# A first feed-forward group of three plain pairs, with the token sums made during its third: five seven-product pairs instead of six

## The chip, the cores and the metric

The kernel runs on one core of a Trainium2 chip. The metric is the device time of one execution in microseconds (us); the time before is the median of three runs. One further execution was taken with the hardware profiler, and every row shown here is from it. A core has a matrix engine (TensorE, called PE in the rows; its weight loads have an engine name of their own, PEld), VectorE (DVE), ScalarE (ACT), GpSimd (POOL), and SyncE (SP), which issues the DMA transfers here. Each engine works through its own list of instructions in order and waits at an instruction until what it needs is there.

## What is computed

One decoder layer on 512 tokens of width 1024, in float32. The part that matters here is the feed-forward block at the end, with `D_FF = 2816`:

```python
h = rmsnorm(x, norm_mix_w[l])
...
x = x + mix @ w_o[l]
h = rmsnorm(x, norm_ffn_w[l])
x = x + (jax.nn.silu(h @ w_gate[l]) * (h @ w_up[l])) @ w_down[l]
return rmsnorm(x, final_norm_w)
```

Ahead of it stand a gated MLP and a sparse attention group, which the change does not touch.

## The kernel before

Every product of float32 values is made from three matmuls (`mm3`, lines 112 to 115): each operand is split into a high part (a copy rounded to `fp32r`, made on ACT, line 81) and a low part (the rest, a subtraction on DVE, line 78), and high times high, high times low and low times high are added up in PSUM. `h2h` and `h2l` are the high and low parts of the normalized tokens, `wg_h`, `wg_l`, `wu_h`, `wu_l` those of gate and up weights, `ah` and `al` those of the activations that go into the down projection.

The 2816 features are cut into 11 pairs of two 128-feature blocks. Pairs are gathered into groups, `FFN_GROUPS = (2, 3, 3, 3)`. For each group the kernel makes gate and up of its pairs one after another and then the down projection of the whole group (`down`). A pair's gate and up is made in one of two ways:

- `plain_pair`: for gate and for up, two feature blocks by eight 128-row slices of the contraction by three matmuls of 512 token columns: 96 matmuls. DVE makes four low parts of weights (128x1024), two products silu(gate) times up (line 710), four sums of 256 columns (line 700) and two low parts of activations. Pair 0 is made in the same way, its first block still inside the stage before.
- `seven_pair`: gate and up, the two halves of the contraction and the two halves of the tokens make a 2x2 block product, done with seven block products (M1 to M7) in place of eight, each of two feature blocks by four slices by three matmuls of 256 columns: 168 matmuls. It needs sums and differences of the weights (`vec2`, line 804), seven low and seven high parts of weights, and sums and differences of the token blocks, `th` and `tl`. M1 takes the plain tokens; M5 is the first that needs `th`.

The token sums are made once by `token_sums` (lines 770 to 788): eight DVE additions and subtractions (lines 776 and 781) of 128x1024, four ACT copies to `th` and four DVE subtractions to `tl`. The call stands after the pairs of group 0, ahead of that group's down projection.

`down` is itself a seven-product scheme (M1, M2, M5, M6, M3, M7, M4 in this order). For every product and pair of the group it splits one 128x512 block of the down weight (`wd0M` to `wd10M`; high on ACT, low on DVE), partly after a difference made in place (lines 924, 927 and 930), and issues 6 matmuls of 512 columns: 42 per pair. After each product but M2, DVE adds two 128x512 results, one per half of 256 tokens, to the residual `x2` (line 890). A result bank (`pA`, `pC`) can be started anew only when its addition has read it, so PE waits on line 890 if DVE is late. M2 has banks of its own (`pB`), kept over all groups.

Raw weights arrive by DMA in three buffers of 1 MB (tag `wr`), used in turn; the split parts go through eight buffers of 128x1024 (tag `wh`), also in turn. A plain pair uses all eight, so the splits of the next pair follow PE at a distance of one pair. The activations of a group stay until its down projection is over; `ACT_HOMES` says in which pool each of them lies. Pool `P` has three buffers and also lends two to `token_sums` for the sums (`tok`).

The order on each engine is made by the framework's scheduler from the order in which the code is written, so instructions of one pair stand among those of the next.

Of the kernel before, what the change touches and what calls it, by code (L numbers as in the profile page):

```python
# [18 lines left out]
P = 128  # L19
# [10 lines left out]
NFB = DFF // P  # L30
C_U, C_V, C_Q, C_KC, C_KS, C_KW, C_G = 0, 512, 1024, 1536, 1792, 2048, 2304
NG = 24
FFN_GROUPS = (2, 3, 3, 3)
SEVEN = (2, 3, 5, 6, 8, 9)
ACT_HOMES = (("xa", "xa", "b8", "P"), ("P", "P", "P", "b8", "xa", "xa"))
START = (("S", 0), ("T", 0), ("W", 0), ("K", 0), ("S", 1), ("T", 1), ("W", 1), ("S", 2), ("K", 1), ("T", 2),
         ("W", 2), ("S", 3), ("K", 2), ("T", 3), ("W", 3), ("K", 3))
BANKS = (3, 2, 2, 1)
# [5 lines left out]
def hybrid_gmlp_nsa_kernel(  # L44
# [18 lines left out]
    def b8(shape, dt, name):  # L63
        return bp.tile(shape, dt, tag="b8", name=name)
# [12 lines left out]
    def sub(o, a, hi, eng=None):  # L77
        return (eng or nc.vector).tensor_tensor(out=o, in0=a, in1=hi.bitcast(F32), op=OP.subtract)  # L78

    def copy_a(o, a):  # L80
        return nc.scalar.activation(o, a, AF.Copy)  # L81
# [35 lines left out]
    def bcast_row(vec, n, name, tag=None):  # L117
        t = (cp if tag else kp).tile([P, DM if tag else n], F32, name=name, tag=tag or name)[:, :n]
        nc.sync.dma_start(t, bass.AP(tensor=vec.tensor, offset=vec.offset, ap=[[0, P], [1, n]]))
        return t  # L120
# [574 lines left out]
    def keep_acts(p, sg, ss):  # L695
        ah, al = act_tile(f"ah{p}"), act_tile(f"al{p}")
        copy_a(ah[:, 0:3], sg[:, 1:4])
        for o, x, y, op in ((ss[:, 0], sg[:, 0], sg[:, 2], OP.add), (ss[:, 2], sg[:, 1], sg[:, 0], OP.subtract),
                            (ss[:, 1], ss[:, 0], sg[:, 1], OP.subtract), (ss[:, 3], sg[:, 3], ss[:, 1], OP.subtract)):
            nc.vector.tensor_tensor(out=o, in0=x, in1=y, op=op)  # L700
        sub(al[:, 0:3], sg[:, 1:4], ah[:, 0:3])
        copy_a(ah[:, 3:7], ss)
        sub(al[:, 3:7], ss, ah[:, 3:7])
        acts.append((ah, al))


    def gate_act(sg, e, pg):
        own = sg[:, 2 * e:2 * e + 2].rearrange("p a c -> p (a c)")
        nc.scalar.activation(own, pg[0], AF.Silu)
        nc.vector.tensor_tensor(out=own, in0=pg[1], in1=own, op=OP.mult)  # L710
# [4 lines left out]
    def gate_up(f, part=None):  # L715
        if part == 0:
            ws = [load_cols(w, 0, KD, f * P, P, f"w{'gu'[a]}{f}", spare=True, behind=mixed[-1])
                  for a, w in ((0, w_gate), (1, w_up))]
            gu[f] = ws, [bank("S", [P, S], f"gu{f}{a}") for a in range(2)]
        elif part is None:  # L720
            raw = wp.tile([P, 2, KD, P], F32, tag="wr", name=f"wgu{f}_r", bufs=NPAIR)
            ws = []
            for a, w in ((0, w_gate), (1, w_up)):
                nc.sync.dma_start(raw[:, a], w[:, f * P:(f + 1) * P].rearrange("(k p) f -> p k f", p=P))
                ws.append(halves(raw[:, a], [KD, P], f"w{'gu'[a]}{f}", last_norm))
            gu[f] = ws, [bank("G", [P, S], f"gu{f}{a}") for a in range(2)]
        cut = slice(0, S) if part is None else slice(part * 256, part * 256 + 256)
        for (hi, lo), z in zip(*gu[f]):
            for k in range(KD):
                mm3(z[:, cut], hi[:, k], lo[:, k], h2h[k // 4][:, k % 4, cut], h2l[k // 4][:, k % 4, cut],  # L730
                    k == 0, k == KD - 1)
        return gu[f][1]
# [17 lines left out]
    def plain_pair(p):  # L750
        sg, ss = t4([P, 4, 256], F32, f"sg{p}"), t4([P, 4, 256], F32, f"ss{p}")
        z = {}
        for a, r in enumerate(pair_raw(p)):
            for kh in range(2):
                hi, lo = halves(r[:, 4 * kh:4 * kh + 4], [4, 256], f"w{'gu'[a]}{p}{kh}")
                for e in range(2):
                    if kh == 0:
                        z[e, a] = bank("G", [P, S], f"gu{p}{a}{e}")
                    for k in range(4):
                        c = slice(e * P, (e + 1) * P)  # L760
                        mm3(z[e, a], hi[:, k, c], lo[:, k, c], h2h[kh][:, k], h2l[kh][:, k],
                            kh + k == 0, kh == 1 and k == 3)
        for e in range(2):
            gate_act(sg, e, (z[e, 0], z[e, 1]))
        keep_acts(p, sg, ss)
# [4 lines left out]
    def token_sums():  # L770
        rs = []
        for a in range(2):
            r = bp.tile([P, 2, 4, 256], F32, tag="P", name=f"tok{a}", bufs=NP)
            for c in range(2):
                cut = slice(c * 256, c * 256 + 256)
                nc.vector.tensor_tensor(out=r[:, c], in0=h2h[a][:, :, cut].bitcast(F32),
                                        in1=h2l[a][:, :, cut].bitcast(F32), op=OP.add)
            rs.append(r)
        y11, y12, y21, y22 = rs[0][:, 0], rs[0][:, 1], rs[1][:, 0], rs[1][:, 1]
        for o, x, y in ((y11, y12, y11), (y12, y22, y12), (y22, y22, y11), (y21, y21, y22)):  # L780
            nc.vector.tensor_tensor(out=o, in0=x, in1=y, op=OP.subtract)
        for a in range(2):
            hi, lo = b8([P, 2, 4, 256], F32R, f"th{a}"), b8([P, 2, 4, 256], F32R, f"tl{a}")
            for c in range(2):
                copy_a(hi[:, c], rs[a][:, c])
                sub(lo[:, c], rs[a][:, c], hi[:, c])
            TH.append(hi)
            TL.append(lo)
# [107 lines left out]
    def down(gi, pairs):  # L896
# [34 lines left out]

        last_group = gi == len(FFN_GROUPS) - 1

# [23 lines left out]
    onw = None  # L957
    for gi, n in enumerate(FFN_GROUPS):
        acts.clear()
        homes[:] = ACT_HOMES[min(gi, 1)]  # L960
        for p in range(p0, p0 + n):
            if p == 0:
                gate_act(sg0, 1, gate_up(1))
                keep_acts(0, sg0, ss0)
            elif p in SEVEN:
                seven_pair(p)
            else:
                plain_pair(p)
        if gi == 0:
            token_sums()  # L970
        if gi == len(FFN_GROUPS) - 1:
            onw = bcast_row(final_norm_w, DM, "onw", tag="wb")
        down(gi, range(p0, p0 + n))
        p0 += n
# [49 lines left out]
```

## Time and profile before

| | us |
|---|---|
| median of three runs | 630.02 |
| the three runs | 630.36, 626.82, 630.02 |
| the profiled execution | 626.75 |
| its span, first to last instruction | 625.0 |
| PE busy in the span | 597.8 |
| DVE busy in the span | 473.0 |
| ACT busy in the span | 329.2 |

The times in the rows are counted from the start of the span. A matmul is pipelined: its row is longer than the distance to the next one, so the pace of PE is read from the starts of matmuls, and that of DVE from the starts of its instructions.

### The profile page before, as it was taken

To read this page: it belongs to the slowest core of one execution; us is meant where nothing else is said; L and a number is where in the kernel's file an instruction comes from. 1 tells how busy PE (TensorE), PEld (TensorE's weight loads), DVE (VectorE), ACT (ScalarE), POOL (GpSimd) and SP (SyncE) were. 2 spreads that over 40 slices of the span, in tenths; PEclk is the share of its full clock that TensorE was granted. 3 is DMA by queue.
4 is the path that set the end of the run, shared out by engine and by line. 5 is a ranking of instruction groups with operands and counts; after the bars stand their busy time and mean duration, and the time that the engine had idled before them with its cause. 6 is when DMAs were issued, how large, how long until landed. Compare 5 with 4: busy or idle time off the path is not lost.

```text
span 625.0 us, 8610 instructions
## 1 busy us (share of the span) xinstructions
PE 597.8 (96%) x3244; PEld 503.6 (81%) x3244; DVE 473.0 (76%) x801; ACT 329.2 (53%) x587; POOL 68.3 (11%) x113
## 2 busy tenths in 40 slices
PE   8999999999999999999958999999999999999994
PEld 5878778787788777888836998888998888998883
DVE  5752778647998967546798898597898597897696
ACT  6653367649877874354341564343464343464354
POOL 3100100015432671000000000000000000000001
PEclk9999999999999999999969999999999999999999
DMA  8451635532000021093004406006415005425003
GB/s 288 144 141 54 179 105 152 184 127 112 1 2 1 1 71 31 17 297 125 1 0 135 136 23 247 1 1 202 136 44 226 0 11 191 136 75 196 1 0 134
DMA packets 52698, 61.38 MB, mean 98 GB/s; under 512 B 3361, under 2 KB 43313, under 8 KB 52658
## 3 DMA queue, kind: packets, MB, share of 16 engines
q1 hardware_dynamic: 52080, 59.80, 29.3%
q10 hardware_dynamic: 578, 1.05, 0.5%
q8 instruction: 25, 0.41, 0.3%
q14 instruction: 15, 0.12, 0.1%
HBM read 58.74 MB, written 2.10 MB: 97 GB/s over the span
## 4 chain that ended last, share of the span: by engine, by line
PE 67%; DVE 19%; DMA 6%; ACT 4%; POOL 2%; issue 2%; POOLq 0%; ACTq 0%; SPq 0%; DVEq 0%
PE gu L114 6%; PE gu L115 6%; PE gu L113 6%; PE o L651 3%; PE ptp L631 3%; PE s L557 3%; DVE x L890 2%; PE po L115 2%; PE po L114 2%; PE gA L115 2%; PE po L113 2%; PE gA L113 2%; PE gA L114 2%; DMA wu_r<-in_w_up_dram 2%; DVE wu_r L804 2%
## 5 line engine op out<-in xcount | busy, mean ns | idle before, releaser
L168 POOL TENSOR_TENSOR rstd_y<-s_y,mhalf 128x1 f32<-128x1 f32 x4 | 3.0, 747 | 355.2 <-DVE s_y L165 350.5
L562 ACT ACTIVATE P<-P,nm 128x128 f32<-128x128 f32 (+3 forms) x64 | 35.5, 559 | 4.8 <-DVE nm L560 4.6
L84 POOL TENSOR_SCALAR P<-P,sm 128x128 f32<-128x128 f32 (+3 forms) x64 | 34.0, 551 | 32.8 <-DVE sm L569 19.6
L560 DVE CUSTOM_DVE_ANT_0 P<-s,maskw 128x128 f32<-128x128 f32 (+3 forms) x64 | 29.5, 481 | 4.2 <-PE s L557 3.6
L651 PE MATMUL o<-PT,Vt 128*128 128x512 f32 x80 | 31.1, 439 | 0.2
L78 DVE TENSOR_TENSOR PT<-ptp,PT 128x512 fp32r<-128x512 f32 x40 | 26.6, 685 | 5.7 <-ACT PT L81 5.5
L113 PE MATMUL gu<-h2h,wg_h 128*128 128x512 f32 x72 | 28.1, 390 | 0.0
L114 PE MATMUL gu<-h2l,wg_h 128*128 128x512 f32 x72 | 28.1, 390 | 0.0
L115 PE MATMUL gu<-h2h,wu_l 128*128 128x512 f32 x72 | 28.0, 389 | 0.0
L115 PE MATMUL gu<-h2h,wg_l 128*128 128x512 f32 x72 | 28.0, 389 | 0.0
L113 PE MATMUL gu<-h2h,wu_h 128*128 128x512 f32 x72 | 28.0, 389 | 0.0
L114 PE MATMUL gu<-h2l,wu_h 128*128 128x512 f32 x72 | 28.0, 389 | 0.0
L631 PE MATMUL ptp<-ident,P 128*128 128x128 f32 x160 | 25.7, 275 | 2.0 <-POOL P L84 1.9
L81 ACT ACTIVATE PT<-ptp 128x512 fp32r<-128x512 f32 x40 | 22.6, 593 | 8.5 <-PE ptp L631 8.1
L557 PE MATMUL s<-KAB,QS 128*128 128x512 f32 (+2 forms) x96 | 27.0, 374 | 0.0
L631 PEld LDWEIGHTS ptp<-ident,P 128*128 128x128 f32 x160 | 19.8, 140 | 7.4 <-POOL P L84 3.2
L890 DVE TENSOR_TENSOR x<-pA,x 128x512 f32<-128x512 f32 x32 | 21.8, 685 | 1.9 <-PE pA L115 1.9
L651 PEld LDWEIGHTS o<-PT,Vt 128*128 128x128 f32 x80 | 14.8, 188 | 7.9 <-ACT PT L81 4.1
L557 PEld LDWEIGHTS s<-KAB,QS 128*128 128x128 f32 x96 | 16.3, 189 | 2.0 <-DVE nm L560 0.3
L81 ACT ACTIVATE sg<-gA 128x512 f32<-128x512 f32 x12 | 7.1, 589 | 19.7 <-PE gA L115 19.7
L804 DVE TENSOR_TENSOR wg_r<-wg_r,wu_r 128x1024 f32<-128x1024 f32 x12 | 14.7, 1223 | 2.8 <-DMA wu_r<-in_w_up_dram 2.4
L81 ACT ACTIVATE ah<-ss 128x1024 fp32r<-128x1024 f32 x11 | 11.6, 1059 | 8.9 <-DVE ss L700 8.9
(735 smaller groups left out, 2088.0 us busy)
## 6 DMA issues: line engine op xcount, KB each, us to landing
wd_r<-in_w_down_dram SPq DMA_DIRECT2D x11, 1024.0 KB, 4.7
wg_r<-in_w_gate_dram SPq DMA_DIRECT2D x10, 1024.0 KB, 7.6
wu_r<-in_w_up_dram SPq DMA_DIRECT2D x10, 1024.0 KB, 5.6
wo_r<-in_w_o_dram SPq DMA_DIRECT2D x8, 512.0 KB, 4.7
x_sb<-in_x_dram SPq DMA_DIRECT2D x4, 512.0 KB, 8.8
wv_r<-in_w_in_dram SPq DMA_DIRECT2D x4, 512.0 KB, 7.2
wu_r<-in_w_in_dram SPq DMA_DIRECT2D x4, 512.0 KB, 4.8
w1k_r<-in_cmp_k_w_dram SPq DMA_DIRECT2D x4, 512.0 KB, 4.2
```

The lines of the kernel that those rows point to most:

```text
L81: return nc.scalar.activation(o, a, AF.Copy)
L84: nc.gpsimd.tensor_scalar(out=o, in0=a, scalar1=s, scalar2=1.0, op0=OP.mult, op1=OP.mult)
L113: nc.tensor.matmul(ps, lhsT=sh, rhs=mh, start=first, stop=False, skip_group_check=more)
L114: nc.tensor.matmul(ps, lhsT=sh, rhs=ml, start=False, stop=False, skip_group_check=more)
L115: nc.tensor.matmul(ps, lhsT=sl, rhs=mh, start=False, stop=last, skip_group_check=more)
L557: nc.tensor.matmul(sb, lhsT=q, rhs=KAB[kv][:, a, b0:b0 + nbr, :n], start=(a == 0), stop=(a == 1))
L560: nc.vector.tensor_tensor_reduce(out=pr, in0=sb[:, br], in1=maskw[:, S - n:], scale=-0.125, scalar=BIG, op0=OP.add, op1=OP.min, accum_out= ...
L562: e = nc.scalar.activation(pr, pr, AF.Exp, bias=nm[b], scale=-1.0, accum_out=sm[b])
L631: nc.tensor.transpose(pt[:, hh], src, ident)
L651: nc.tensor.matmul(of, lhsT=Vt[:, b0 + br, j, kv], rhs=PTs[u][:, a], start=(first and a == 0), stop=False)
L804: nc.vector.tensor_tensor(out=o, in0=x, in1=y, op=op)
L890: nc.vector.tensor_tensor(out=x2[t][:, c], in0=src, in1=x2[t][:, c], op=OP.add)
```

## The change

Groups are now of 3, 3, 2 and 3 pairs. Pair 2 moves into group 0 and is made plain; pairs 3 and 4 (seven) and 5 (plain) make group 1, pairs 6 (seven) and 7 (plain) group 2, and 8 and 9 (seven) and 10 (plain) group 3, as before. So six pairs of seven products become five. `token_sums` is called after pair 1, ahead of pair 2. The homes of the first group's activations get two entries more, both in pool `P`.

```diff
-FFN_GROUPS = (2, 3, 3, 3)
-SEVEN = (2, 3, 5, 6, 8, 9)
-ACT_HOMES = (("xa", "xa", "b8", "P"), ("P", "P", "P", "b8", "xa", "xa"))
+FFN_GROUPS = (3, 3, 2, 3)
+SEVEN = (3, 4, 6, 8, 9)
+ACT_HOMES = (("xa", "xa", "b8", "P", "P", "P"), ("P", "P", "P", "b8", "xa", "xa"))
...
             else:
                 plain_pair(p)
-        if gi == 0:
-            token_sums()
+            if p == 1:
+                token_sums()
         if gi == len(FFN_GROUPS) - 1:
             onw = bcast_row(final_norm_w, DM, "onw", tag="wb")
         down(gi, range(p0, p0 + n))
```

On DVE at the end of pair 1, before the change. `sg1`, `ss1`, `al1` are pair 1's gated results, their sums and their low part, `wd0M6` the split of pair 0's down weight for M6, `pA00` and `pA01` the two banks of M1.

```order
L710 TENSOR_TENSOR sg1_2782<-gu111_2863,sg1_2782 128x512
L78 TENSOR_TENSOR wd0M6_3011<-wd0_r_2940,wd0M6_3011 128x512
L700 TENSOR_TENSOR ss1_2783<-sg1_2782 128x256
L78 TENSOR_TENSOR wd1M6_3015<-wd1_r_2942,wd1M6_3015 128x512
L700 TENSOR_TENSOR ss1_2783<-ss1_2783,sg1_2782 128x256
L78 TENSOR_TENSOR al1_2909<-sg1_2782,ah1_2908 128x768
L700 TENSOR_TENSOR ss1_2783<-sg1_2782,ss1_2783 128x256
L776 TENSOR_TENSOR tok0_2918<-h2h0_1179,h2l0_1181 128x1024 x2
L78 TENSOR_TENSOR al1_2909<-ss1_2783,ah1_2908 128x1024
L776 TENSOR_TENSOR tok1_2921<-h2h1_1180,h2l1_1182 128x1024 x2
L781 TENSOR_TENSOR tok0_2918<-tok0_2918 128x1024
L890 TENSOR_TENSOR x2_1_1172<-pA00_2950,x2_1_1172 128x512
```

On DVE at the same place, of the change. `wu21` is the last quarter of pair 2's weights, `wd0M1` the split of pair 0's down weight for M1.

```order
L710 TENSOR_TENSOR sg1_2782<-gu111_2863,sg1_2782 128x512
L700 TENSOR_TENSOR ss1_2783<-sg1_2782 128x256
L78 TENSOR_TENSOR wu21_l_3035<-wu2_r_2944,wu21_h_3034 128x1024
L700 TENSOR_TENSOR ss1_2783<-ss1_2783,sg1_2782 128x256
L78 TENSOR_TENSOR al1_2909<-sg1_2782,ah1_2908 128x768
L700 TENSOR_TENSOR ss1_2783<-sg1_2782,ss1_2783 128x256
L776 TENSOR_TENSOR tok0_2918<-h2h0_1179,h2l0_1181 128x1024 x2
L78 TENSOR_TENSOR al1_2909<-ss1_2783,ah1_2908 128x1024
L776 TENSOR_TENSOR tok1_2921<-h2h1_1180,h2l1_1182 128x1024 x2
L781 TENSOR_TENSOR tok0_2918<-tok0_2918 128x1024
L78 TENSOR_TENSOR wd0M1_3082<-wd0_r_3076,wd0M1_3082 128x512
```

The sums keep their place behind pair 1's gated results. Before, the splits for M1, M2, M5 and M6 stood ahead of them and the first addition of M1's result (line 890) among them; now pair 2's weights stand ahead of them, and the first splits for M1 among them.

On DVE at the end of group 0's down projection, of the change: `pA00` and `pA01` are here the banks of M4, the last product, `wd2M4` the split of pair 2's down weight for it, `w3M1` and `w3M5` the weights of pair 3's first and second product.

```order
L78 TENSOR_TENSOR wd2M4_3275<-wd2_r_3080,wd2M4_3275 128x512
L890 TENSOR_TENSOR x2_0_1171<-pA00_3091,x2_0_1171 128x512
L890 TENSOR_TENSOR x2_0_1171<-pA01_3101,x2_0_1171 128x512
L78 TENSOR_TENSOR w3M1_l_3305<-wg3_r_3300,w3M1_h_3304 128x1024
L804 TENSOR_TENSOR wg3_r_3300<-wg3_r_3300,wu3_r_3302 128x1024
L804 TENSOR_TENSOR wu3_r_3302<-wu3_r_3302 128x1024
```

On DVE at the same place between the groups of three pairs before the change (group 1 to pair 5; `pA10` and `pA11` hold M7 and then M4, `pC11` M3):

```order
L890 TENSOR_TENSOR x2_1_1172<-pC11_3774,x2_1_1172 128x512
L890 TENSOR_TENSOR x2_0_1171<-pA10_3703,x2_0_1171 128x512
L78 TENSOR_TENSOR w5M1_l_3915<-wg5_r_3910,w5M1_h_3914 128x1024
L890 TENSOR_TENSOR x2_0_1171<-pA11_3713,x2_0_1171 128x512
L804 TENSOR_TENSOR wg5_r_3910<-wg5_r_3910,wu5_r_3912 128x1024
L890 TENSOR_TENSOR x2_0_1171<-pA10_3703,x2_0_1171 128x512
L804 TENSOR_TENSOR wu5_r_3912<-wu5_r_3912 128x1024
```

The first product's weights, which between groups of three pairs stand ahead of the last three additions, stand behind all of them at the end of the new group 0.

## Rows read from the trace of the kernel before

**Rows 1.** The page, part 1: busy time, share of the span, instructions.

```profile
PE 597.8 (96%) x3244; PEld 503.6 (81%) x3244; DVE 473.0 (76%) x801; ACT 329.2 (53%) x587; POOL 68.3 (11%) x113
```

**Rows 2.** PE's waits, 300 to 346 us: waiting instruction, releaser, us, times, longest.

```profile
PE pA L113 <- DVE x L890: 6.8, 2, 4.0
PE gC L113 <- ACT w2M_h L81: 1.9, 1, 1.9
PE gC L115 <- DVE w2M_l L78: 0.8, 1, 0.8
```

**Rows 3.** Windows: busy time (count) of PE, PEld, DVE, ACT, POOL; PEclk, DMA share, GB/s.

```profile
318.00:328.40 10.40, 6.38 (x17) 4.01 (x15) 10.40 (x13) 4.23 (x4) 0.00 (x0) 0.51 0.00 0
342.00:345.40 3.40, 3.19 (x15) 3.19 (x16) 2.18 (x3) 1.89 (x2) 0.00 (x0) 0.51 0.02 5
```

**Rows 4.** PE's timeline, first matmuls of pieces: start, duration (us), engine, line, out<-in, shapes.

```profile
303.20 0.39 PE L113 MATMUL gu<-h2h,wu_h 128*128 128x512 f32 x1
...
305.93 0.39 PE L113 MATMUL pA<-wd0M,ah 128*128 128x512 f32 x1
...
352.14 0.28 PE L113 MATMUL gA<-th,w2M_h 128*128 128x256 f32 x1
...
357.90 0.28 PE L113 MATMUL gA<-th,w2M_h 128*128 128x256 f32 x1
...
360.78 0.28 PE L113 MATMUL gA<-h2h,w3M_h 128*128 128x256 f32 x1
...
380.93 0.40 PE L113 MATMUL gu<-h2h,wg_h 128*128 128x512 f32 x1
...
402.72 0.39 PE L113 MATMUL pA<-wd2M,ah 128*128 128x512 f32 x1
...
431.61 0.28 PE L113 MATMUL gA<-h2h,w5M_h 128*128 128x256 f32 x1
...
452.40 0.28 PE L113 MATMUL gA<-h2h,w6M_h 128*128 128x256 f32 x1
...
473.81 0.40 PE L113 MATMUL gu<-h2h,wg_h 128*128 128x512 f32 x1
```

**Rows 5.** DVE's timeline behind pair 1, 306 to 313 us (idle before, releaser in brackets).

```profile
306.13 0.69 DVE L710 TENSOR_TENSOR sg<-gu,sg 128x512 f32<-128x512 f32 x1 [0.32 <-PE gu L115]
306.73 0.68 DVE L78 TENSOR_TENSOR wd0M<-wd_r,wd0M 128x512 fp32r<-128x512 f32 x1
307.33 0.42 DVE L700 TENSOR_TENSOR ss<-sg 128x256 f32<-128x256 f32 x1
307.67 0.68 DVE L78 TENSOR_TENSOR wd1M<-wd_r,wd1M 128x512 fp32r<-128x512 f32 x1
...
308.61 0.95 DVE L78 TENSOR_TENSOR al<-sg,ah 128x768 fp32r<-128x768 f32 x1
309.48 0.42 DVE L700 TENSOR_TENSOR ss<-sg,ss 128x256 f32<-128x256 f32 x1
309.81 2.35 DVE L776 TENSOR_TENSOR tok<-h2h,h2l 128x1024 f32<-128x1024 f32 x2
312.08 1.22 DVE L78 TENSOR_TENSOR al<-ss,ah 128x1024 fp32r<-128x1024 f32 x1
```

**Rows 6.** DVE's timeline, two starts of a seven-product pair; last row: the tile wu_r's landings.

```profile
331.17 0.68 DVE L78 TENSOR_TENSOR wd0M<-wd_r,wd0M 128x512 fp32r<-128x512 f32 x1
...
337.28 1.23 DVE L804 TENSOR_TENSOR wg_r<-wg_r,wu_r 128x1024 f32<-128x1024 f32 x1
338.54 1.23 DVE L804 TENSOR_TENSOR wu_r<-wu_r 128x1024 f32<-128x1024 f32 x1
340.93 1.23 DVE L78 TENSOR_TENSOR w2M_l<-wu_r,w2M_h 128x1024 fp32r<-128x1024 f32 x1 [1.17 <-ACT w2M_h L81]
...
427.32 1.23 DVE L78 TENSOR_TENSOR w5M_l<-wg_r,w5M_h 128x1024 fp32r<-128x1024 f32 x1 [0.94 <-ACT w5M_h L81]
...
DMA to landing us min/median/max: 5.2/5.6/5.7
```

## The prediction

> **What bounds the kernel now.** I read the page's busy times first: PE is busy for 597.8 of 625.0 us [rows 1], so the time is PE's work plus PE's gaps. A pipelined matmul's busy time hides its pace, so I read the pace from starts: twelve matmuls of 512 columns lie between 303.20 and 305.93, 0.2275 us each; 48 of 256 columns lie between 352.14 and 357.90, 0.120 us each [rows 4]. Then I went piece by piece through the feed-forward part and set each piece against this pace.
>
> - Plain pair 4, 96 matmuls, 380.93 to 402.72: 21.79 us. No gap.
> - Seven-product pair 3, 168 matmuls, 360.78 to 380.93: 20.15 us, against 168 x 0.120 = 20.16. No gap.
> - Down projection of three pairs (126 matmuls, 28.67 us at this pace) and pair 5 (20.16), 402.72 to 452.40: 49.68 us, 0.85 more than the pace. Pair 6, 452.40 to 473.81: 21.41, so 1.25 more [rows 4].
> - Down projection of group 0 (84 matmuls, 19.11) and pair 2 (20.16), 305.93 to 360.78: 54.85 us against 39.27. Here 15.6 us are lost.
>
> The view of waits names them: 6.8 us in two waits for the addition of line 890, then 1.9 and 0.8 for the weights of pair 2 [rows 2], 9.5 in all. The other 6.1 are slow matmuls: the granted clock is 0.51, so the lower level of 1.2 GHz, from 318.0 to 328.4 and from 342.0 to 345.4 [rows 3], each behind such waits. The cause stands in DVE's timeline: behind pair 1 come the token sums [rows 5], and the additions that free PE's banks are queued among and behind them. DVE is the bound of this stretch, and PE of all others.
>
> **The change part by part.** *What goes.* The 15.6 us of this stretch. What becomes of DVE's debt there is worked out below as a new loss.
>
> *Pair 2 plain instead of seven.* 72 matmuls fewer, but wider: 21.79 - 20.16 = +1.6 us on PE. The Trainium skill ("TensorE: Matmul & The Clock Gate", section on the back-to-back issue gap) has a sustained pace of 131 ns at 512 columns and 81 at 128; halfway by columns that is about 98 at 256, an estimate from that page. By it a plain pair would be 96 x 131 = 12.6 us, a seven-product one 168 x 98 = 16.5, and this term -3.9 in place of +1.6. The measured starts differ from that page by 70%, and the measurement decides.
>
> DVE loses ten instructions and ACT six with pair 2's seven products; neither is on the path there, so I count nothing for them. The DMA bytes are the same.
>
> *Pair 2 itself, with the sums beside it.* The listings show pair 2's four weight splits on DVE ahead of the sums; the last starts when PE leaves pair 1, and PE needs it three quarters into pair 2, 16 us later. So pair 2 should run without a gap, from 305.93 to 327.72. The four ACT copies to `th` lie beside it; the last waits in ACT's queue behind two splits for M2, whose `wh` buffers PE frees three quarters into pair 2, near 322.3. That makes it ready near 324.7, about when DVE comes to it.
>
> *Group 0's down projection.* DVE's cost per instruction, by distance of starts: 0.60 us at 512 columns, 0.34 at 256, 0.87 at 768, 1.14 at 1024 [rows 5]. From its start at 306.13 to the last addition of the new group 0 DVE has: three products of line 710 (1.8), seven sums of line 700 (2.4), four low parts of activations (4.0), pair 2's last split (1.1), 12 sum instructions (13.6), 21 splits (12.6), differences of lines 924, 927, 930 (3.4 + 3.6) and 14 additions (8.4): 50.9 us. PE has 21.79 + 28.67 = 50.5 in the same time. So they are nearly even, and DVE enters the down projection with no lead. Laying the listed order out by these costs, I get DVE at the second line 710 of pair 2 at 328.1, PE through M2 at 336.3 (0.4 late), waiting 0.75 for pair 1's split for M5, which stands behind three differences, and about 0.8 in M6 and M3; M4 ends at 358.1 instead of 356.4. Loss: 1.7. Bounds: 0.4 (50.9 - 50.5) and 6.8, the waits on line 890 now [rows 2].
>
> *Start of pair 3.* In the steady state the first product's weights are split at 427.32, four us before PE wants them at 431.61 [rows 4, 6]. Now that split stands behind the last two additions, the very last of which waits for PE's last matmul: addition 358.3 to 358.9, split to 360.05. PE issues two matmuls of M1 and waits 1.8 us. Then the chain that pair 2 shows, two differences and an ACT copy (337.28, 338.54, 340.93 [rows 6]), gives M5's high part at 363.45 and its low part at 364.6, while PE ends M1 at 362.75: 0.7 and 1.0 us. M6 and M2 lose another 0.3. Loss: 3.8. Bounds: 0.85, the steady state, and 8.8, all of the 15.6 but the waits on line 890.
>
> *Which pairs follow which.* Pairs 3 and 4 now stand as 2 and 3 did; pair 6, which lost 1.25 as second of its group, becomes a first. I credit half: -0.6 (0 to -1.25).
>
> *Group of two pairs.* DVE has 14 additions and 14 splits (16.8) and the differences (2.3 + 2.4), 21.5 us, against 19.1 on PE. But the listing of the change has the splits for M1, M2 and M5 and all differences done before pair 7 ends, which covers the 2.4 missing. The up weights of pair 8 take the buffer of pair 6's down weights; DVE last reads that about 10.9 us into the down projection. A load lands 5.6 us later [rows 6], at 16.5, and DVE, ACT and DVE bring M5's weights to PE at about 22.0, when it has finished M1 (19.1 + 2.9). I take +0.3, bounds 0 and 2.7 (what pair 2 loses there now, rows 2).
>
> **The sum:** -15.6 + 1.6 + 1.7 + 3.8 - 0.6 + 0.3 = -8.8 us. On the profiled execution's 626.75 that is 618.0. The median of the runs shown, 630.02, lies 3.3 above it. If that difference sits elsewhere, the new median is 621.2; if it sits in the waits that go, 618.0. I take the middle, 619.5.
>
> **The rivals.** *The lower clock comes back.* Behind waits of 1.9 and 0.8 us within four us the clock was at 0.51 for 3.4 us [rows 2, 3], which cost 1.7. The new waits at the start of pair 3, 1.8, 0.7 and 1.0 within seven us, are like them, but more spread out. One such stretch gives -7.1; the full 6.1 of now gives -2.7. The middle is about 622 on the median's scale. The Trainium skill (the same page, on how the clock gate bites in real kernels) has the clock fall behind long gaps of PE; the waits here were short and it fell, so its rule does not exclude this.
>
> *DVE holds its lead.* If the engines slide so that both new losses shrink to the lower bounds (0.4 and 0.85), the sum is -13.4 and the time 613.3 to 616.6. For it: the balance of 50.9 against 50.5. Against it: the fixed order of the last split.
>
> *The page's pace.* With -3.9 for pair 2 the sum is -14.3, some 613. The rows exclude it all but wholly.
>
> *DVE's debt is larger than 50.9 (slower).* That sum has no time for hand-overs from ACT. DVE idles 0.94 and 1.17 for such copies [rows 6]. With 0.6 us in each of the 21 splits the debt is 13 us, all of it PE's waits on line 890 or on splits, since DVE has no lead. Add the 6.1 of low clock and 3.8 at pair 3: 22.9 in place of 5.5, sum +8.6, time 635 to 638. It decides from a new loss of 15 us on. Against it: in the 20 us behind pair 1 DVE waits nearly nowhere now [rows 5], as the copies run ahead while DVE is late.
>
> **How the numbers follow.** Forecast 0.66, low clock 0.14, DVE's lead 0.10, the page's pace 0.01, larger debt 0.09, of which half ends slower. A difference of 1%, 6.3 us, is about what can be told from none here. Faster by more: the forecast nearly whole (0.60), lead and page (0.11), a third of the low clock (0.05): 0.76. Slower by more: 0.05. Same: 0.19. The range runs from 612.5 (the lead, on the profiled execution's scale, with a margin) to 627.5 (low clock in full, -2.7 on the median). The scale of the runs, 3.3 us, is in it.
>
> **What would show it.** PE's waits on line 890 in group 0 gone or under 1 us; pair 2 from about 305.9 to 327.7 without a gap; `gA` of pair 3 waiting 1 to 2 us for `w3M_l`, then `gC` for `w3M_h` and `w3M_l`; pair 3 ending near 382; clock 1.00 throughout group 0; down projection of pairs 6 and 7 at about 19.1 us. Wrong: waits on line 890 of several us in the new group 0, clock near 0.5 there, or pair 8 starting with waits for `wu_r`.

## The result and the profile after

The changed kernel takes 622.39 us (median of 4 runs, 620.21 to 622.87), the kernel before 628.96 (4 runs, 626.82 to 630.36). The ratio is 0.9892 with a 95% interval of 0.9852 to 0.9932: faster, by about 1.1%. Whether it is more or less than 1% the interval (0.7 to 1.5%) leaves open. The profiled execution took 620.21 us, its span is 618.5. That is 6.5 below the span before; the prediction had 8.8.

The page's busy times (part 1) and the granted clock of the 40 slices, after the change:

```profile
PE 597.3 (97%) x3172; PEld 498.2 (81%) x3172; DVE 463.5 (75%) x791; ACT 324.5 (52%) x581; POOL 68.3 (11%) x113
...
PEclk9999999999999999999999999999999999999998
```

PE has 72 matmuls fewer and the same busy time [rows 1]: a plain pair has fewer but wider ones. What changed is the gaps, and the stretches at half the clock, in which busy time grows without more work. PE's waits from 300 to 372 us, the part that lost 15.6 us before (columns as in [rows 2]):

```profile
PE gA L115 <- DVE w3M_l L78: 1.3, 1, 1.3
PE gC L113 <- ACT w3M_h L81: 1.0, 1, 1.0
PE gC L115 <- DVE w3M_l L78: 0.8, 1, 0.8
PE pC L114 <- DVE wd1M L78: 0.3, 1, 0.3
PE pC L113 <- ACT wd1M L81: 0.2, 1, 0.2
```

The 6.8 us for line 890 [rows 2] are gone, and three waits for the first weights of pair 3 have come. The window that had half the clock before [rows 3] now lies in pair 2:

```profile
318.00:328.40 10.40, 10.40 (x48) 8.61 (x47) 10.40 (x12) 6.15 (x9) 0.00 (x0) 1.00 0.00 0
```

PE is busy for all of it at clock 1.00, with DVE busy throughout as well. The first matmuls of the pieces, in PE's timeline (compare [rows 4]):

```profile
306.55 0.39 PE L113 MATMUL gu<-h2h,wg_h 128*128 128x512 f32 x1
...
328.31 0.39 PE L113 MATMUL pA<-wd0M,ah 128*128 128x512 f32 x1
...
359.23 0.39 PE L113 MATMUL gA<-h2h,w3M_h 128*128 128x256 f32 x1
...
383.83 0.28 PE L113 MATMUL gA<-h2h,w4M_h 128*128 128x256 f32 x1
...
404.62 0.40 PE L113 MATMUL gu<-h2h,wg_h 128*128 128x512 f32 x1
...
426.41 0.39 PE L113 MATMUL pA<-wd3M,ah 128*128 128x512 f32 x1
...
476.59 0.40 PE L113 MATMUL gu<-h2h,wg_h 128*128 128x512 f32 x1
...
498.37 0.39 PE L113 MATMUL pA<-wd6M,ah 128*128 128x512 f32 x1
...
538.75 0.28 PE L113 MATMUL gA<-h2h,w9M_h 128*128 128x256 f32 x1
...
559.64 0.40 PE L113 MATMUL gu<-h2h,wg_h 128*128 128x512 f32 x1
```

Set against the same pace as in the prediction (0.2275 us for 512 columns, 0.120 for 256), each difference of two starts gives one term:

| piece | starts | at pace | lost | term of the sum | predicted |
|---|---|---|---|---|---|
| pair 2, plain, instead of seven products | 21.76 | 21.8 | 0 | +1.6 | +1.6 |
| old stretch of 15.6 us | | | | -15.6 | -15.6 |
| down projection of the new group 0 | 30.92 | 28.67 | 2.25 | +2.2 | +1.7 |
| pair 3 | 24.60 | 20.16 | 4.44 | +4.4 | +3.8 |
| pair 4 (1.25 lost there before, as pair 6) | 20.79 | 20.16 | 0.63 | -0.6 | -0.6 |
| down projection and pair 6 (0.85 before) | 50.18 | 48.83 | 1.35 | +0.5 | 0 |
| down projection of two pairs and pair 8 (0.78 before) | 40.38 | 39.27 | 1.11 | +0.3 | +0.3 |
| pair 9 (0.80 before) | 20.89 | 20.16 | 0.73 | -0.1 | 0 |

They add up to -7.2 (-7.15 before rounding). The untouched part ahead ended 0.6 later in this execution (pair 1 ends at 306.55 against 305.93), which leaves the -6.5 of the two spans.

DVE's timeline in the same part (compare [rows 5, 6]):

```profile
310.49 2.35 DVE L776 TENSOR_TENSOR tok<-h2h,h2l 128x1024 f32<-128x1024 f32 x2
...
324.22 2.35 DVE L78 TENSOR_TENSOR tl<-tok,th 128x1024 fp32r<-128x1024 f32 x2
...
328.62 0.68 DVE L710 TENSOR_TENSOR sg<-gu,sg 128x512 f32<-128x512 f32 x1
...
352.08 0.69 DVE L78 TENSOR_TENSOR wd0M<-wd_r,wd0M 128x512 fp32r<-128x512 f32 x1
352.69 0.69 DVE L78 TENSOR_TENSOR wd1M<-wd_r,wd1M 128x512 fp32r<-128x512 f32 x1
```

The token sums run from 310.5 to 326.6, beside pair 2. DVE comes out of it without a lead: its last product of pair 2 starts at 328.62, when PE has already begun the down projection. The last two rows are the splits for M4, the last product. They read a raw buffer each, and what follows them is the start of pair 3. The timeline of SP, ACT and DVE there:

```profile
352.80 0.37 SPq L746 DMA_DIRECT2D wg_r<-in_w_gate_dram  x1
...
353.40 0.39 SPq L746 DMA_DIRECT2D wu_r<-in_w_up_dram  x1
...
358.11 1.06 ACT L81 ACTIVATE w3M_h<-wg_r 128x1024 fp32r<-128x1024 f32 x1 [2.79 <-DMA wg_r<-in_w_gate_dram]
359.12 0.69 DVE L890 TENSOR_TENSOR x<-pA,x 128x512 f32<-128x512 f32 x1 [1.36 <-PE pA L115]
...
359.73 1.22 DVE L78 TENSOR_TENSOR w3M_l<-wg_r,w3M_h 128x1024 fp32r<-128x1024 f32 x1
...
361.11 1.22 DVE L804 TENSOR_TENSOR wg_r<-wg_r,wu_r 128x1024 f32<-128x1024 f32 x1 [0.17 <-DMA wu_r<-in_w_up_dram]
```

Both loads of pair 3 are issued behind those splits. The gate weights land when ACT starts, 358.1 (5.3 us after the issue), the up weights when DVE can start its difference, 361.1 (7.7 us). So the load and the split's place behind the last addition (359.12) come within a microsecond of each other, and the experiments had to tell them apart.

### The profile page after: what moved, and what is told of

It is laid out like the page before. It is cut to its first block, busy times and chain, and to the rows that moved or that the text cites. A ratio compares the mean times of both kernels' runs of the same rounds, so it can differ in the third digit from the quotient of the medians.

```text
span 618.5 us, 8448 instructions
## 1 busy us (share of the span) xinstructions
PE 597.3 (97%) x3172; PEld 498.2 (81%) x3172; DVE 463.5 (75%) x791; ACT 324.5 (52%) x581; POOL 68.3 (11%) x113
## 4 chain that ended last, share of the span: by engine, by line
PE 63%; DVE 20%; DMA 8%; ACT 4%; POOL 2%; issue 2%; POOLq 0%; ACTq 0%; SPq 0%; DVEq 0%
PE gu L114 6%; PE gu L115 6%; PE gu L113 6%; DMA wu_r<-in_w_up_dram 4%; PE o L651 3%; PE ptp L631 3%; PE s L557 3%; PE po L115 2%; PE po L114 2%; PE po L113 2%; DVE wu_r L804 2%; DVE x L890 2%; PE gA L115 1%; DVE wg_r L804 1%; PE gA L114 1%
## 5 line engine op out<-in xcount | busy, mean ns | idle before, releaser
L113 PE MATMUL gu<-h2h,wg_h 128*128 128x512 f32 x88 | 34.3, 390 | 0.0
L114 PE MATMUL gu<-h2l,wg_h 128*128 128x512 f32 x88 | 34.3, 390 | 0.0
L115 PE MATMUL gu<-h2h,wg_l 128*128 128x512 f32 x88 | 34.2, 389 | 0.0
L113 PE MATMUL gu<-h2h,wu_h 128*128 128x512 f32 x88 | 34.2, 389 | 0.0
L114 PE MATMUL gu<-h2l,wu_h 128*128 128x512 f32 x88 | 34.2, 389 | 0.0
L115 PE MATMUL gu<-h2h,wu_l 128*128 128x512 f32 x88 | 34.2, 389 | 0.0
L890 DVE TENSOR_TENSOR x<-pA,x 128x512 f32<-128x512 f32 x32 | 21.8, 687 | 3.7 <-PE pA L115 3.6
L81 ACT ACTIVATE wu_h<-wu_r 128x1024 fp32r<-128x1024 f32 x10 | 10.6, 1062 | 22.5 <-PE gu L114 7.2
L115 PEld LDWEIGHTS gu<-h2h,wg_l 128*128 128x128 f32 x88 | 16.5, 188 | 3.5
L115 PEld LDWEIGHTS gu<-h2h,wu_l 128*128 128x128 f32 x88 | 16.5, 188 | 3.4
L114 PEld LDWEIGHTS gu<-h2l,wu_h 128*128 128x128 f32 x88 | 16.5, 188 | 3.4
```

Of the source, the lines that this page charges most:

```text
L113: nc.tensor.matmul(ps, lhsT=sh, rhs=mh, start=first, stop=False, skip_group_check=more)
L114: nc.tensor.matmul(ps, lhsT=sh, rhs=ml, start=False, stop=False, skip_group_check=more)
L115: nc.tensor.matmul(ps, lhsT=sl, rhs=mh, start=False, stop=last, skip_group_check=more)
L890: nc.vector.tensor_tensor(out=x2[t][:, c], in0=src, in1=x2[t][:, c], op=OP.add)
```

## The experiments

Each kernel was timed beside the kernel before; the ratios are to that. A "loss" is, as above, the difference of two starts less the pace.

### Where do the token sums cost?

**Both kernels without the sums.** `TH` and `TL` are views of the normed activations, so the sums and the splits of them are left out, and the seven-product pairs compute something else:

```diff
-        rs = []
         for a in range(2):
...
+            TH.append(h2h[a].rearrange("p k (c n) -> p c k n", c=2))
+            TL.append(h2l[a].rearrange("p k (c n) -> p c k n", c=2))
```

In the kernel before:

> The kernel before without the token sums: the plain tokens are handed to the five products that need sums, so the 12 DVE instructions and 4 ACT copies are left out and the output is another. Theory (DVE's 13.6 us of sums, queued ahead of the additions that free PE's banks, make the loss of 15.6 us between pair 1 and pair 3): that stretch loses about 1 us, no wait on line 890, clock 1.00 there, time 13 to 15 us less than before, about 615. Rival (the change gained because pair 2 became plain and the groups were cut anew; the sums lie beside PE's work anyhow): within 2 us of before.

Measured: 615.32 us, ratio 0.9788 [0.9766, 0.9810]. The stretch from pair 1's end to pair 3 loses 1.25 us in place of 15.6, and there is no wait for line 890. All but 1.25 of that loss came from the sums. That they act through DVE is told by the waits on DVE's line 890, which go; the four ACT copies to `th` are left out with them here. Pair 3, which lost nothing before, now loses 1.0.

In the kernel after:

> The changed kernel without the token sums, left out in the same way (the output is another). Theory (the 6.7 us still lost in group 0 and at the start of pair 3 are what is left of the same debt): the down projection of group 0 loses under 0.5 us and the start of pair 3 about 1, so 5 to 6 us less than the changed kernel, about 617. Rival: these losses come from a group of three plain pairs and from the loads of raw weights, whatever DVE does: within 1.5 us of the changed kernel.

Measured: 616.90 us, ratio 0.9815 [0.9783, 0.9848]; the span is 614.0. Group 0's down projection loses 0.2 and pair 3 0.64. So the change doesn't hide the sums: they cost 13.2 us before (628.51, the time before in this comparison, less 615.32) and still some 5 after (4.5 by the spans, 5.5 by the medians). The two kernels without sums differ by 1.6 us in their medians and 0.5 in their spans; their intervals overlap, so the price of the plain pair rests on the starts above.

**Pair 2 plain, groups and sums as before:**

```diff
-SEVEN = (2, 3, 5, 6, 8, 9)
+SEVEN = (3, 5, 6, 8, 9)
```

> The kernel before with pair 2 plain and nothing else changed (five seven-product pairs, groups of 2, 3, 3, 3, sums behind pair 1). Theory: the waits on line 890 (6.8 us) and the slow matmuls behind them stay; only the waits at the start of pair 2 (2.7 and some low clock) go, for 1.6 us more of matmuls: 0 to 4 us less than before, about 627. Rival (fewer seven-product pairs relieve DVE and that is the gain): about the changed kernel, 622.

Measured: 625.27 us, ratio 0.9946 [0.9927, 0.9965]. PE's waits, 300 to 346 us, are one row:

```profile
PE pA L113 <- DVE x L890: 6.2, 2, 3.3
```

The waits for the weights of a seven-product pair 2 are gone, but the waits on line 890 stay, and with them the half clock from 318 to about 327. Fewer seven-product pairs alone are not what helps; the cover for the sums is.

### Is pair 2 the right cover?

**The sums one pair earlier.** In the kernel before, at the end of pair 0 in place of the end of group 0:

```diff
                 plain_pair(p)
-        if gi == 0:
-            token_sums()
+            if p == 0:
+                token_sums()
```

> The kernel before with its groups and six seven-product pairs, the token sums called behind pair 0 instead of behind pair 1. Theory: DVE makes them where it now idles for ACT and PE (about 262 to 290 us), M1 to M6 are split before the down projection of group 0, and that stretch loses 1 to 3 us; up to 2 us may be lost in pair 0 instead: 9 to 14 us less than before, about 617, so better than the changed kernel without its plain pair. Rival (the regrouping is what helps): within 2 us of before.

Measured: 614.92 us, ratio 0.9786 [0.9765, 0.9806], as fast as with no sums at all. The first and the last row of the sums in DVE's timeline:

```profile
268.90 1.22 DVE L776 TENSOR_TENSOR tok<-h2h,h2l 128x1024 f32<-128x1024 f32 x1
...
284.02 2.36 DVE L78 TENSOR_TENSOR tl<-tok,th 128x1024 fp32r<-128x1024 f32 x2
```

They lie beside pair 0, which PE works on until 285. The busy times of pairs 0 and 1 say why (columns as in [rows 3]), first in the kernel before:

```profile
266.00:306.00 40.00, 39.53 (x200) 33.46 (x198) 22.86 (x30) 16.05 (x22) 0.00 (x0) 1.00 0.50 162
```

and then with the sums there:

```profile
266.00:307.00 41.00, 40.52 (x207) 34.41 (x207) 34.99 (x42) 19.87 (x26) 0.00 (x0) 1.00 0.52 166
```

DVE, the third engine of the row, was busy for 22.9 of 40 us, so it had 17 us idle beside PE; the 13.6 us of sums fit, and PE loses nothing. The down projection and pair 2, from 306.72 to 347.22, lose 1.2.

**The same place in the kernel after** (`if p == 0:` in place of `if p == 1:`):

> The changed kernel with its token sums behind pair 0 instead of pair 1. Theory (only DVE's debt from the sums was lost, and the plain pair 2 costs its matmuls): the losses of group 0 and pair 3 fall from 6.7 to about 1 us, as without sums; about 616.5, and 1.6 us more than the kernel before with the sums at the same place. Rival (a first group of three plain pairs has a worth of its own): equal to that kernel or faster, 615 or less.

Measured: 616.32 us, ratio 0.9797 [0.9763, 0.9832]. The down projection of group 0 loses 0.2 and pair 3 0.78, as without the sums. The loads of pair 3, in the view of SP's queue:

```profile
348.63 0.37 SPq L746 DMA_DIRECT2D wg_r<-in_w_gate_dram  x1
351.27 0.37 SPq L746 DMA_DIRECT2D wu_r<-in_w_up_dram  x1
```

They go out 4.2 and 2.1 us earlier than in the changed kernel, though the down projection starts 2.2 us later in this execution (330.50): counted from its start, 6.4 and 4.3 us earlier. DVE has split M4's raw weights earlier. The sums' price at pair 3 (3.8 us: 4.44 less 0.64), then, comes in large part through the loads; the fourth raw buffer, below, takes away 2.1 of it. The kernel is 1.4 us slower than the one with the sums at pair 0 and the old groups, of the size of the plain pair's 1.6, though the intervals overlap.

**With the sums at pair 0, pair 1 as a seven-product pair too** (old groups, `SEVEN = (1, 2, 3, 5, 6, 8, 9)`):

> The kernel before with the sums behind pair 0 and pair 1 made with seven products too (seven pairs of seven products). By PE's matmuls alone 1.6 us less than with pair 1 plain, 613. If DVE, which then has about 20 us of pair 1 beside 20 of PE and the sums just ahead, falls behind, PE waits in pair 1 and in the down projection of group 0 as in the kernel before: 616 to 622. I expect the second, at about 617, since the sums and pair 1 together take 34 us of DVE.

Measured: 626.55 us, ratio 0.9960 [0.9944, 0.9976], 11.6 us above the kernel with pair 1 plain. My expectation had the direction and missed the size by about 10. PE's timeline shows waits in pair 1 and again in pair 2:

```profile
290.38 0.39 PE L113 MATMUL gC<-th,w1M_h 128*128 128x256 f32 x1 [2.16 <-ACT w1M_h L81]
...
291.97 0.39 PE L115 MATMUL gC<-th,w1M_l 128*128 128x256 f32 x1 [1.08 <-DVE w1M_l L78]
...
337.16 0.39 PE L113 MATMUL gC<-th,w2M_h 128*128 128x256 f32 x1 [2.30 <-ACT w2M_h L81]
```

Behind both the granted clock falls (0.88 from 286 to 300, 0.73 from 338 to 350). Beside pair 1 DVE has no time left: it is busy for 13.92 of the 14 us from 286 to 300. At pair 2 the up weights come last as well: their load goes out at 327.93, and DVE's first difference waits for it until 333.48. So the idle time of DVE beside a plain pair can be spent once, on the sums or on seven products; how much of the loss at pair 2 is DVE's lateness and how much the load this run does not tell apart.

### What holds up pair 3?

**The split ahead of the last additions.** If the prediction's cause is right, M1's low part, made ahead of the last two additions of group 0, takes most of the 1.3 us away, and the waits behind it shrink. In `down`, behind M4 (the rest of the edit only hands these weights on to pair 3):

```diff
...
         product("M4", 1, "A", False, lambda r: r[:, 1, 0], t4_of)
-        if not last_group:
+        if gi == 0:
+            raw = pair_raw(3)
+            ahead[3] = raw, halves(raw[0][:, 0:4], [4, 256], "w3M1", mark=ahead)
+            for c in range(2):
+                after(accumulate(c, 0, banks["A", c]), ahead["lo"])
+        elif not last_group:
             add(0, 0, "A")
```

> The changed kernel with the split of pair 3's first weights held ahead of the last two additions of group 0 on DVE, by an ordering alone. The prediction's step (the split waits behind these additions): the wait of 1.3 us in M1 goes and the chain to M5 starts earlier, 1 to 2 us less than the changed kernel. Rival (the gate weights of pair 3 landed only at about 358.1 and the up weights at 361.1, since their buffers were read late by DVE; the order is not what counts): within 0.6 us of the changed kernel, the two waits of M5 as long as before.

Measured: 621.29 us, ratio 0.9875 [0.9850, 0.9900]. By the medians that is 1.1 us less than the changed kernel, by the spans 1.0 more (619.5 against 618.5), and the intervals overlap: the times do not decide between the two expectations, so the rows must. PE's waits, 300 to 372 us:

```profile
PE gC L113 <- ACT w3M_h L81: 1.8, 1, 1.8
PE gA L115 <- DVE w3M_l L78: 0.8, 1, 0.8
PE gC L115 <- DVE w3M_l L78: 0.8, 1, 0.8
PE gA L113 <- ACT w3M_h L81: 0.5, 1, 0.5
```

3.8 us in place of 3.0. The two waits in M1 (0.45 and 0.76) are together as long as the one before, 1.27. The timeline of ACT and DVE has the split ahead of the additions (lines have moved by two), and it starts only 0.24 us earlier than in the changed kernel:

```profile
358.40 1.06 ACT L81 ACTIVATE w3M_h<-wg_r 128x1024 fp32r<-128x1024 f32 x1 [3.09 <-DMA wg_r<-in_w_gate_dram]
...
359.49 1.22 DVE L78 TENSOR_TENSOR w3M_l<-wg_r,w3M_h 128x1024 fp32r<-128x1024 f32 x1 [3.25 <-ACT w3M_h L81]
360.63 1.28 DVE L892 TENSOR_TENSOR x<-pA,x 128x512 f32<-128x512 f32 x2
361.83 1.22 DVE L806 TENSOR_TENSOR wg_r<-wg_r,wu_r 128x1024 f32<-128x1024 f32 x1
```

DVE stands idle for 3.25 us for ACT's copy, and that waits for the gate weights, whose load goes out at 352.79 as in the changed kernel. It lands 0.3 us later in this execution (ACT starts at 358.40, not 358.11); with equal landing the order alone would be worth about 0.5 us, an estimate from these starts. For M1's split the two causes coincide, and taking the order away uncovers the load. The edit has a price as well: both additions now stand between the split and M5's first difference, which starts at 361.83 in place of 361.11, and PE's wait for M5's high part is 1.84 in place of 0.98. So this run shows that the order is not the whole cause; it does not show what M5's waits would be without the order. Now the clock falls too, in the window behind these waits:

```profile
365.40:371.20 5.80, 4.95 (x26) 4.74 (x27) 4.50 (x4) 2.06 (x4) 0.00 (x0) 0.71 0.00 0
```

**A fourth raw buffer.** If the load is the cause, a buffer that is free early takes it away. The memory for it comes from the gated results' buffers, four of which become three:

```diff
-NHALF, NPAIR, NXA = 8, 3, 2
+NHALF, NPAIR, NXA = 8, 4, 2
...
-    n_t4 = 4
+    n_t4 = 3
```

> The changed kernel with four raw weight buffers instead of three, and three buffers instead of four for the gated results to make room. Late loads: pair 3's gate weights land long before, its up weights about 3 us earlier, in the buffer freed first; pair 3 loses about 1.5 us instead of 4.4, 2 to 3 us less than the changed kernel in the profile. Rival (DVE's order and its debt make the loss): within 1 us of the changed kernel. The down projection keeps its loss of about 2 us by both.

Measured: 615.17 us, ratio 0.9776 [0.9749, 0.9804]: 7 us by the medians and 4.9 by the spans, where 2 to 3 were expected. SP's queue and PE's waits:

```profile
309.96 0.37 SPq L746 DMA_DIRECT2D wg_r<-in_w_gate_dram  x1
353.70 0.37 SPq L746 DMA_DIRECT2D wu_r<-in_w_up_dram  x1
```

```profile
PE gC L115 <- DVE w3M_l L78: 0.8, 1, 0.8
PE gC L113 <- ACT w3M_h L81: 0.5, 1, 0.5
```

The gate weights are loaded 43 us earlier, the wait for M1's low part is gone, and pair 3 loses 2.3 in place of 4.4. The rest was in no term of mine: pair 4 loses 0 in place of 0.63, the down projection with pair 6 0.2 in place of 1.35, that with pair 8 0.2 in place of 1.11, pair 9 0 in place of 0.73. The steady-state losses of about a microsecond at every group, which the prediction took as given, were late loads as well. With 0.25 less in group 0's down projection the pieces gain 5.8; the part ahead ended 0.9 later, which makes the 4.9.

**Only the three result buffers** (`n_t4 = 3` alone), to see which half of that edit counts:

> The changed kernel with only the other half of the run with four raw buffers: three buffers for gated results, raw buffers still three. By the theory that the fourth raw buffer gave the whole gain: within 1.5 us of the changed kernel, the waits at pair 3 as long as there. Rival (the different buffers moved DVE's order to the better): about 615.

Measured: 621.94 us, ratio 0.9892 [0.9870, 0.9915], as the changed kernel. The gain is the raw buffer's. The waits at pair 3 stay, 3.5 us in place of 3.0: with the same times of issue, both loads land 0.3 us later than in the changed kernel's rows (after 5.5 and 7.9 us, not 5.2 and 7.6). Behind them the clock falls as it did with the split ahead:

```profile
365.40:371.20 5.80, 5.04 (x29) 4.84 (x29) 4.55 (x4) 2.55 (x4) 0.00 (x0) 0.71 0.00 0
```

DVE's order here is the changed kernel's, so it was not the ordering edit that brought the clock down there.

**The fourth raw buffer in the kernel before** (both edits):

> The kernel before with four raw buffers only, the sums where they were. Theory: the waits on line 890 (6.8 us) and the slow matmuls behind them stay, the waits at the start of pair 2 shrink to under 1 us and 3 us go at the later groups: 4 to 7 us less than before, about 623. Rival (late loads were the root in the kernel before too): 617 or less.

Measured: 624.33 us, ratio 0.9930 [0.9906, 0.9953], 4 us. The later groups' losses go, but the waits for the additions are still there:

```profile
PE pA L113 <- DVE x L890: 7.2, 2, 4.3
```

The waits at the start of pair 2 stay too (1.7 and 0.8 us), where I had expected under 1. So there are two troubles, and either stays when the other is taken away: the sums in the wrong place, and loads that wait for a buffer.

### Both removed

The sums at pair 0, the old groups with six seven-product pairs, and the fourth raw buffer:

> Both cures together: the kernel before with the sums behind pair 0 and four raw weight buffers (three for gated results). If the two losses are separate (the debt of the sums; raw weights that land late at every change from down projection to seven-product pair), the gains add: the sums alone gave 614.9, the fourth buffer took 2.1 us at pair 3 and about 3 more at the later groups of the changed kernel, so about 610. Rival (both remove the same lateness of DVE): 613 to 615, as with the sums alone.

Measured: 609.02 us, ratio 0.9684 [0.9666, 0.9703], the fastest kernel of the study, 13 us below the changed one. The view of PE's waits from 300 to 372 us is empty. PE's starts of the down projection, of pair 3 and of pair 4:

```profile
307.26 0.39 PE L113 MATMUL pA<-wd0M,ah 128*128 128x512 f32 x1
...
346.77 0.28 PE L113 MATMUL gA<-h2h,w3M_h 128*128 128x256 f32 x1
...
366.93 0.40 PE L113 MATMUL gu<-h2h,wg_h 128*128 128x512 f32 x1
```

39.51 us against 39.27 at pace, and 20.16 against 20.16. The plain pair's cover isn't needed.

Not tried: the sums still later, at the end of the new group 0. Their buffers and the third pair's activations don't fit into pool `P` together.

## Why the prediction was right, and where it was not

The measured 622.39 us lies inside the range (612.5 to 627.5), 2.9 above the forecast of 619.5, and the kernel is faster, as was most likely. On the scale of the profiled execution the forecast was 618.0, measured 620.2; by the medians 621.2, measured 622.4. Point by point:

- **The stretch of 15.6 us goes.** Right. Its cause, DVE's sums in front of the additions that free PE's banks, is shown by the kernel without sums (1.25 left) and by moving them (1.2 left).
- **Pair 2 plain, without a gap, +1.6.** Right: 21.76 us, and the starts keep the pace of plain pair 4 before.
- **Group 0's down projection, +1.7.** Measured 2.25. That DVE has no lead is what the trace shows: the second line 710 of pair 2 was laid out at 328.1 and came at 328.62, the last addition at 358.3 and came at 359.12. The sum of 50.9 us behind it was wrong, though: it has 14 additions, and there are 12, two behind each of six products. With 12 it is 49.7, less than PE's 50.5. DVE works without a pause from 306.75 to 354.6 even so, and PE waits for single splits (0.2 to 0.3 us each): the order of DVE's work counts here, not its sum alone. The same count of 14 stands in the sum for the group of two pairs.
- **Start of pair 3, +3.8.** Measured 4.44, and here the step that failed is the cause. The prediction said that M1's split "stands behind the last two additions" and took the loads as landed. The order does hold the split, but the load of the gate weights lands so late (358.1) that with the split ahead it starts only 0.24 us sooner, about 0.5 had the load landed alike. The up weights land at 361.1, and M5's difference waits for them. The size came out near by luck: two causes of the same length lay over each other. The code has it: group 0's three raw down weights fill all three raw buffers until M4's splits have read them, so the loads of pair 3 go out behind those. The prediction followed that chain for pair 8 (raw buffer free, 5.6 us of load, splits) and not for pair 3.
- **Which pairs follow which, -0.6.** Measured -0.6. The pair behind the next down projection, counted at 0, lost 0.5 more. Both are late loads, as the fourth raw buffer shows.
- **Group of two pairs, +0.3.** Measured +0.3.
- **The lower clock comes back (rival).** Not in the profiled execution: the clock is 1.00 through group 0 and pair 3. The mean clock of its whole span is 0.996; that of the three other runs is 0.990, and they took 622.4 to 622.9 us, 2.2 to 2.7 more. So these runs have some more time at the lower clock. The kernels with the split ahead and with three result buffers show such a stretch at exactly the place that the rival named, with like waits, both behind loads that landed 0.3 us later. Whether it lies there in the changed kernel's other runs stays open, as only one of them has rows. By the time alone the rival is not excluded: its middle of 4.9 us less than before is 621.9 on the profiled execution's scale, which the prediction called the median's, and 623.4 on the forecast's own. The measured 622.39 lies between this and 619.5.
- **DVE holds its lead, and DVE's debt is larger (rivals).** Neither: the down projection and pair 3 lost 6.7 us together, where these had 1.25 and over 15. The first one's sum is -13.05 by its own terms, not -13.4. **The page's pace (rival).** The plain pair took 21.76 us, not 12.6.

The expected gain of -8.8 became -6.5 by four small terms: 0.5 in the down projection, 0.6 at pair 3, 0.5 at pair 6 and the 0.6 ahead of the change.

## What to carry to other kernels

A block of work for an engine with spare time belongs where that engine's idle time is measured beside the bounding engine: in the kernel before the sums cost 13 us at the end of the first group and nothing beside its first pair, in the changed one about 5 beside the third pair and nothing beside the first. At the start of a stage, follow every load back to the instruction that frees its buffer: a late split on DVE delays not only what stands behind it but the load that is to come into the buffer it reads. When a wait has an instruction order as its cause, look for what else ends within a microsecond of it; taking away the later of two such causes gains only the distance between them.

## What the runs showed of the hardware

In the changed kernel two loads of 1 MB issued 0.6 us apart land 5.2 and 7.6 us after their issue, and the engines that wait for them start 0.1 us later. A gate load with no other beside it, issued at 481.05 in the same run, landed after 5.1. The summary of the transfers in the changed kernel between 350 and 365 us, in 40 slices, with the loads' median landing:

```profile
GB/s 0 0 0 22 0 0 0 0 0 0 117 194 268 336 385 388 388 385 366 352 350 352 350 352 350 350 341 350 350 350 347 344 350 347 276 98 0 0 0 0
...
wu_r<-in_w_up_dram SPq DMA_DIRECT2D x1, 1024.0 KB, 7.6
```

The loads that follow one another here (a third goes out at 356.28) share about 350 GB/s; the first lands about as early as the one alone, the second 2.4 us later. With the fourth raw buffer, where the up weights go first, it is they that land in 5.4 us, and the load issued 0.6 us behind them in 7.8. The Trainium skill ("DMA: Bandwidth & Descriptors", Specifications) gives about 358 GB/s as the limit of HBM for one core. The plateau of 341 to 352 here lies just under it, but the five slices of 366 to 388 ahead of the plateau lie above, so this row does not show it as a hard limit.

Whether PE's clock falls behind a few short waits is a close thing. In the changed kernel waits of 1.27, 0.98 and 0.76 us between 359.7 and 366.2 left it at 1.00; with the split ahead, 0.45, 0.76, 1.84 and 0.76 brought it to 0.71 from 365.4 to 371.2, so part of that window at 1.2 GHz; with three result buffers, 0.43, 0.98, 1.29 and 0.76 did the same. The Trainium skill ("TensorE: Matmul & The Clock Gate", A second HAM failure mode: psum-queue depth-cycling) says that brief idle times between groups of matmuls can make the clock swing too; the rows of the second and third kernels agree, the first shows that it need not.
